# Thirty adaLN blocks go from VectorE to TensorE, and the list that places them is written anew

## The chip, the cores and the metric

The kernel runs on one core of a Trainium2 chip. The metric is the device time of one execution in microseconds (us): the median of the runs. Five engines with instruction streams of their own work side by side: TensorE (PE in the rows; PEld are its weight loads), VectorE (DVE), ScalarE (ACT), GpSimd (POOL) and SyncE (SP), which issues nearly all DMAs of this kernel in order.

## The reference

A two-layer trunk on 256 tokens of 2048 channels, all in float32. Layer 0 is a state-space layer (S5), then keys and values are made once, then layer 1 is attention. Every norm is modulated by the vector `c`: a shift, a scale and, at the end of a layer, a gate, each of 2048 values.

```python
def reference(x, c, ...):
    c_act = silu(c)
    # layer 0
    shift, scale, gate = split(c_act @ mod_w[0] + mod_b[0], 3)
    h = modulate(rmsnorm(x, norm_g[0]), shift, scale)
    x = x + gate * s5_mixer(h, ...)                 # u, z = h @ w_in; scan; GLU; @ w_out
    # shared keys and values
    kv_shift, kv_scale = split(c_act @ kv_mod_w + kv_mod_b, 2)
    h_kv = modulate(rmsnorm(x, kv_norm_g), kv_shift, kv_scale)
    shared = nsa_shared_kv(h_kv, w_kv, ...)         # compressed, selected, window
    # layer 1
    shift, scale, gate = split(c_act @ mod_w[1] + mod_b[1], 3)
    h = modulate(rmsnorm(x, norm_g[1]), shift, scale)
    x = x + gate * nsa_mixer(h, w_qg, w_o, *shared) # queries, gates, attention, @ w_o
    return rmsnorm(x, final_norm_g)
```

The products `c_act @ mod_w` are the adaLN products: 16 blocks of 128 columns for each shift, scale or gate, 128 blocks in all (48 of layer 0, 32 of keys and values, 48 of layer 1). A block is 1 MB of weights that meets one vector.

## The kernel before

**Projections.** A projection (`project`, L231) makes 128 output columns by 256 tokens: 16 weight blocks of 128x128, each split by ScalarE into a high part (`hi`, L202) and by VectorE into the rest (`lo`, L203), and 48 matmuls into one PSUM tile `acc` (L227 to L229). Weights come by SP into `raw` tiles of 512 KB, from a ring of 8 that all weight loads and adaLN loads share.

**adaLN blocks.** Shift and scale of layer 0 are summed by TensorE at the start. The other 96 blocks can go two ways. `pe_mod` takes two blocks (a pair) to TensorE: four DMAs of 512 KB, 32 matmuls of 32 columns into `macc` (L157; the profile has two records for each), a copy by ScalarE (`msum`, L160), two matmuls with ones (L162, four records), two short ScalarE results in `modv`. `dve_mod` takes one block to VectorE: two DMAs of 512 KB (L142) and two halves, each one multiply with a running sum against the broadcast `cact` (L144); the second halves' sums lie in `modw`. `mod_finish` adds the two parts and the bias. `NA, NB = 0, 2` give TensorE 18 blocks (the gate of layer 0 and two of layer 1: 9 pairs) and VectorE 78 (156 halves).

**Stages.** In program order: modulation of layer 0 and half of u; then S5 (the rest of u, the halves of z, `scan_in`, `scan_run`, which is a serial recurrence on VectorE at L608 to L611, `scan_local`, `scan_out`, `y_turn`, for two halves of the channels); GLU (16 projections of `yhl`); output (16 projections of `ghl`; VectorE adds to x at L722 and sums the squares into `tot`, L244); the norm of `x` (`rms_scale`, L247 to L253: a matmul with ones, square root on ScalarE, reciprocal on VectorE, L252) and `norm_mod` to `hkv`; kv (24 projections of `hkv`, the compressions, and the first queries row by row); q (16 projections of queries, the first 4 already made); attention (16 heads, with the z projections between) and the output projection.

**What sets the order.** The Python program is written out by hand, and each engine keeps the order that results. After most steps `fill()` (L555) takes the next string of `PLAN` and does what its letters say: u or z halves, `m` for a pair on TensorE, `d` for a block on VectorE, `c` and `q` for compressions and query rows. What `PLAN` hasn't done in time, loops at the end of a stage do.

Of the kernel before, what the change touches and what calls it, by code (L numbers as in the profile page):

```python
# [8 lines left out]
F32 = mybir.dt.float32  # L9
# [9 lines left out]
KT = 16  # L19
# [18 lines left out]
# columns of the adaLN products, by blocks of 128: 0..47 layer 0, 48..95 layer 1, 96..127 keys and values.  # L38
# Blocks 0..31 come first; of the rest TensorE takes some (weights as they lie) and VectorE the others (turned round).
NA, NB = 0, 2  # L40
# [3 lines left out]
QN = 4    # blocks of the queries that are computed row by row  # L44


def spread(n, slots, a=0):
    """n things over slots a .. slots"""
    r = [0] * slots
    for i in range(n):  # L50
        r[a + i * (slots - a) // n] += 1
    return r


NR = 8    # blocks of u that are computed row by row
SK = 2
# what fills each slot of the program: u, z halves of blocks, m, d modulation (TensorE, VectorE),
# c pieces of the compression, q rows of the queries
PLAN = [
# [4 lines left out]
    "cmd", "mdqq", "dq", "mddq", "dqq", "mdq", "dq", "mddqq", "dq", "mdq", "mqq", "mq", "mq", "d", "d", "",  # L64
    "d", "d", "", "d", "", "", "d", "d", "dd", "d", "", "", "", "d", "d", "d", "", "d", "d", "dd", "", "d",
    "d", "d", "", "d", "dd", "", "",
# [4 lines left out]
def trunk_kernel(ctx, tc, xT, crow, ccol, vec, m0n, mn, mt, w_ur, w_in, w_glu, w_out, w_kv, w_qr, w_q, w_g,  # L71
# [24 lines left out]
    # ---------------------------------------------------------------- constants  # L96
# [34 lines left out]
    # ---------------------------------------------------------------- adaLN products  # L131
    modv = pool.tile([128, 128], F32, name="modv")
    modw = pool.tile([128, 80], F32, name="modw")                     # columns 48 ..
# [41 lines left out]
    # columns of modv: 0..47 layer 0, 48..95 layer 1, 96..127 kv  # L175
    def mod_finish(col, n):
        """Those of the columns col .. col + n that VectorE has summed, in two parts."""
        t = [x for x in range(col, col + n) if x in DVE_MODS]
        if t:
            c = slice(t[0], t[-1] + 1)  # L180
            assert len(t) == t[-1] + 1 - t[0]
            nc.vector.tensor_add(modv[:, c], modv[:, c], modw[:, c.start - 48:c.stop - 48])
            nc.vector.tensor_add(modv[:, c], modv[:, c], vv_("mb", c.start, c.stop))

    # ---------------------------------------------------------------- projections
# [8 lines left out]
    def split_w(r, n):  # L194
        """The first n of the eight blocks in r, four by four."""
# [11 lines left out]
    class Act:  # L207
        """A matrix [2048 channels, 256 tokens] as a high and a low part."""
# [22 lines left out]
    def project(src, act):  # L231
        """The sums [128 columns, 256 tokens]."""
# [13 lines left out]
    def rms_scale(tot):  # L246
        """1 / sqrt(mean square over channels), for every token, on all partitions."""  # L247
# [7 lines left out]
    def norm_mod(xt, rstd, scol, bcol, act, ks=range(KT)):  # L255
        """act = split of (x * rstd) * S + B."""
# [7 lines left out]
    # ---------------------------------------------------------------- layer 0: modulation and u  # L264
    # (the first NR blocks of u, row by row of w_in as the modulation of the rows comes in)
# [38 lines left out]
    # ---------------------------------------------------------------- S5 tables  # L304
# [10 lines left out]
    def exact_exp(dst, src):  # L315
        """e^src to float32's accuracy: 2^k times a polynomial of what is left."""
# [40 lines left out]
    # powers a^1..a^4: [128, 64, 4] real, imaginary  # L357
# [20 lines left out]
    # coef  # L378
# [6 lines left out]
    # coef * a^(3-j): [128, 64, 4]  # L385
# [13 lines left out]
    # a^4 for the chunk recurrence  # L399
# [25 lines left out]
    def outer(dst0, dst1, mr, mi, wr, wi, sub):  # L425
        """dst0 = mr*wr - mi*wi; dst1 = mi*wr + mr*wi, or with sub, mi standing for -mi:
        dst0 = mr*wr + mi*wi; dst1 = mi*wr - mr*wi.  [128, 16 gp, 4, 16]"""
# [13 lines left out]
    for s in (2, 3, 0, 1):  # L441
# [11 lines left out]
        # C a^0 .. C a^3 side by side  # L453
# [5 lines left out]
        # K_d[c_in, c_out] = Re(C a^d Bbar) of the pairs (h = (l, q), b) at partitions (q, b, c_in)  # L459
# [16 lines left out]
        # the input tables turned round, in place: (b, j, c) on partitions, [h, r, g2, n]  # L476
# [12 lines left out]
    # ---------------------------------------------------------------- the rest of u, z, and the scan, in two halves  # L489
    # (halves of the channels; tokens t = 4 k + j are held in the order (j, k) until the end of the layer)  # L490
    ucm = pool.tile([128, KT, 4, 64], F32, tag="zz", name="ucm")
    U = pool.tile([128, KT, 4, 64], F32, tag="uu", name="U")          # (e, j, c), [b, (g2, hl), k]
# [14 lines left out]
    def u_turn(f):  # L507
        """Half of u, (g, e, c) on partitions, to (e, j, c) on partitions."""
# [53 lines left out]
    def scan_in(f):  # L562
        """Inputs of the recurrence over chunks."""
# [38 lines left out]
    def scan_run(f):  # L602
        """The recurrence over chunks."""
# [9 lines left out]
    def scan_local(f, tz):  # L613
        """What comes out of a chunk from its own inputs, in place of U."""
# [14 lines left out]
    def scan_out(f, cts):  # L629
        """The part of y that the states carry, on to U."""  # L630
        VH = VV[f]
        ys = VH[:, 0:8].rearrange("p h r b k -> p (h r b k)").rearrange("p (b g k) -> p b g k", g=4, k=64)
        for q in range(2):
# [10 lines left out]
            for g2 in range(2):  # L644
# [3 lines left out]
                else:  # L648
                    # VectorE is at the recurrence of the other half
# [5 lines left out]
    ycm = U                                                            # (g, e, c), [b, j, k]  # L655

    def y_turn(f):
        """Back to channels (g, e, c) on partitions, through the GELU."""
# [44 lines left out]
    # ---------------------------------------------------------------- GLU  # L703
# [26 lines left out]
    while ndve[0] < 32 - NA:  # L730
        dve_mod()
    mod_finish(96, 32)

    # ---------------------------------------------------------------- shared keys and values
# [46 lines left out]
    def cmp_piece(e, i):  # L781
        """A quarter of the first product of a compression, then the rest of it."""
# [56 lines left out]
    # (queries of the first heads, row by row of their weights as the modulation of the rows comes in)  # L839
# [49 lines left out]
    # masks  # L889
    masks = []  # L890
    for qh in range(2):
# [3 lines left out]
        # cmp: 16 n + 31 <= pos  # L895
# [12 lines left out]
    # gates, token-major [128 tokens, half, (branch, head)]  # L908
# [21 lines left out]
    # half of the gate: the SiLU of z is taken as (1 + tanh(z / 2)) * z, twice its value  # L930
# [10 lines left out]
    # ---------------------------------------------------------------- attention, head by head  # L941
    att = pool.tile([128, 4096], F32, tag="zz", name="att")
    for h in range(16):
        kv = h // 4
        pn = []
        for qh in range(2):
# [12 lines left out]
            # sections: cmp 16 | sel n | win n  # L959
# [22 lines left out]
        # transposed probabilities  # L982
# [36 lines left out]
    # ---------------------------------------------------------------- output projection, final norm  # L1019
# [26 lines left out]
def _lay_out(i):  # L1046
# [10 lines left out]
    def pairs(a):  # L1057
        # groups (b, g2, gpl) -> [g2, (b, gpl), ...]
        return a.reshape((16, 2, 4) + a.shape[1:]).swapaxes(0, 1).reshape((2, 64) + a.shape[1:])
# [30 lines left out]
    lam = np.stack([pairs(i["ssm_lam_re"][0]), pairs(i["ssm_lam_im"][0])])          # [2, g2, gp, n]  # L1090
# [32 lines left out]
```

## Time and profile before

| | |
|---|---|
| device time, median of 3 runs | 1364.43 us (1359.98 to 1368.99) |
| profiled execution: span | 1368.1 us; no time apart from its span is given |
| PE busy | 1267.0 us, 93% |
| VectorE busy | 1068.3 us, 78% |
| ScalarE busy | 681.7 us, 50% |
| DMA | 332.88 MB, mean 243 GB/s |

The profiled span lies 3.7 us above the median and inside the runs. Busy time of PE includes stretches at the lower of its two clock levels; in the rows by window, PEclk is the granted clock as a part of full speed.

### The profile page before, as it was taken

The page shows a single profiled execution, that of the slowest core. Times are in us where ns is not written, and L with a number is a line of the kernel's source. Part 1 is how long each engine was busy: PE and PEld are TensorE (multiplying, and loading weights), DVE is VectorE, ACT ScalarE, POOL GpSimd, SP SyncE. Part 2 cuts the span into 40 slices and gives each one's busy share as a digit, 9 for nine tenths or more (in the row PEclk, how much of TensorE's full clock was granted, in tenths as well). Part 3 has the DMA queues.
Part 4 walks back from the last instruction along what each step waited for, and adds up shares of the span by engine and source line. Part 5 has one row for each costly group of instructions (what it writes and reads, how often), then busy time and mean ns, then how long its engine had stood idle before and what let it go on. Part 6 is the DMA issues. An engine that isn't in the chain of part 4 may idle for free.

```text
span 1368.1 us, 31424 instructions
## 1 busy us (share of the span) xinstructions
PE 1267.0 (93%) x12270; PEld 1200.6 (88%) x12270; DVE 1068.3 (78%) x2612; ACT 681.7 (50%) x1439; POOL 42.5 (3%) x71
## 2 busy tenths in 40 slices
PE   2799979989999999997998999999999999999995
PEld 2678779878888999986997999999999999999995
DVE  5998318999997898889877878776878777777665
ACT  3345544423356555544453545555555555555653
POOL 1000500001001000000000000000000000000001
PEclk9999989999999999997899999999999999999998
DMA  9799966649788999985887888876555444444541
GB/s 359 275 347 336 316 200 200 205 172 336 242 300 299 321 357 318 327 305 187 293 303 248 277 295 289 274 253 227 170 193 194 165 144 141 159 142 161 186 155 62
DMA packets 94055, 332.88 MB, mean 243 GB/s; under 512 B 12785, under 2 KB 13025, under 8 KB 92881
## 3 DMA queue, kind: packets, MB, share of 16 engines
q1 hardware_dynamic: 91792, 321.45, 68.3%
q0 software_dynamic: 2112, 9.42, 2.1%
q8 instruction: 96, 1.57, 0.5%
q14 instruction: 55, 0.44, 0.1%
HBM read 326.10 MB, written 4.72 MB: 242 GB/s over the span
## 4 chain that ended last, share of the span: by engine, by line
PE 68%; DVE 15%; DMA 12%; issue 3%; ACT 2%; SPq 0%; DVEq 0%; ACTq 0%
PE acc L229 18%; PE acc L227 18%; PE acc L228 18%; DMA raw<-in_mt_dram 6%; DVE lo L203 3%; DMA raw<-in_w_in_dram 3%; DVE raw L144 2%; PE macc L157 2%; PE s L957 1%; DVE stab L608 1%; DMA mraw<-in_m0n_dram 1%; PE op L1008 1%; DVE stab L610 1%; PE kp L467 1%; DVE stab L609 1%
## 5 line engine op out<-in xcount | busy, mean ns | idle before, releaser
L202 ACT ACTIVATE hi<-raw 128x512 fp32r<-128x512 f32 x640 | 400.9, 631 | 466.1 <-PE acc L228 395.9
L203 DVE TENSOR_TENSOR lo<-raw,hi 128x512 fp32r<-128x512 f32 x640 | 435.0, 690 | 146.8 <-ACT hi L202 143.6
L228 PE MATMUL acc<-hq,hi 128*128 128x256 f32 x960 | 274.9, 286 | 0.0
L229 PE MATMUL acc<-hq,lo 128*128 128x256 f32 x960 | 271.5, 284 | 2.5 <-DVE lo L203 2.3
L227 PE MATMUL acc<-hq,hi 128*128 128x256 f32 x960 | 273.2, 285 | 0.4 <-ACT hi L202 0.4
L144 DVE SCALAR_TENSOR_TENSOR raw<-raw,cact 128x1024 f32<-128x1024 f32 x156 | 190.1, 1220 | 57.0 <-DMA raw<-in_mt_dram 56.6
L229 PEld LDWEIGHTS acc<-hq,lo 128*128 128x128 f32 x960 | 180.5, 189 | 5.4 <-DVE lo L203 3.9
L228 PEld LDWEIGHTS acc<-hq,hi 128*128 128x128 f32 x960 | 180.9, 188 | 3.7 <-issue 3.3
L227 PEld LDWEIGHTS acc<-hq,hi 128*128 128x128 f32 x960 | 180.9, 188 | 1.3 <-issue 0.7
L229 PE MATMUL acc<-h,lo 128*128 128x256 f32 x384 | 114.0, 297 | 12.7 <-DVE lo L203 12.3
L229 PE MATMUL acc<-hkv,lo 128*128 128x256 f32 x384 | 114.2, 299 | 5.1 <-DVE lo L203 4.6
L227 PE MATMUL acc<-hkv,hi 128*128 128x256 f32 x384 | 112.5, 295 | 4.9 <-ACT hkv L260 4.9
L227 PE MATMUL acc<-h,hi 128*128 128x256 f32 x384 | 113.5, 296 | 1.0 <-ACT hi L202 1.0
L228 PE MATMUL acc<-hkv,hi 128*128 128x256 f32 x384 | 111.9, 294 | 0.8 <-DVE hkv L261 0.8
L228 PE MATMUL acc<-h,hi 128*128 128x256 f32 x384 | 111.6, 291 | 0.0
L229 PEld LDWEIGHTS acc<-h,lo 128*128 128x128 f32 x384 | 76.1, 198 | 17.4 <-DVE lo L203 14.0
L229 PEld LDWEIGHTS acc<-hkv,lo 128*128 128x128 f32 x384 | 77.3, 202 | 7.6 <-DVE lo L203 7.2
L227 PEld LDWEIGHTS acc<-hkv,hi 128*128 128x128 f32 x384 | 77.3, 202 | 5.8 <-ACT hkv L260 5.8
L227 PEld LDWEIGHTS acc<-h,hi 128*128 128x128 f32 x384 | 76.1, 198 | 5.3 <-issue 2.5
L228 PEld LDWEIGHTS acc<-hkv,hi 128*128 128x128 f32 x384 | 77.4, 202 | 1.4 <-DVE hkv L261 1.4
L157 PE MATMUL macc<-mraw,cz 128*32 128x128 f32 x1600 | 59.0, 300 | 18.9 <-DMA mraw<-in_m0n_dram 17.9
L228 PEld LDWEIGHTS acc<-h,hi 128*128 128x128 f32 x384 | 76.1, 198 | 0.1
(312 smaller groups left out, 2829.6 us busy)
## 6 DMA issues: line engine op xcount, KB each, us to landing
raw<-in_mt_dram SPq DMA_DIRECT2D x156, 512.0 KB, 5.6
raw<-in_w_z_dram SPq DMA_DIRECT2D x96, 512.0 KB, 3.7
mraw<-in_m0n_dram SPq DMA_DIRECT2D x64, 512.0 KB, 7.8
raw<-in_w_in_dram SPq DMA_DIRECT2D x48, 512.0 KB, 6.1
raw<-in_w_kv_dram SPq DMA_DIRECT2D x48, 512.0 KB, 5.2
mraw<-in_mn_dram SPq DMA_DIRECT2D x36, 512.0 KB, 6.6
raw<-in_w_glu_dram SPq DMA_DIRECT2D x32, 512.0 KB, 6.3
raw<-in_w_out_dram SPq DMA_DIRECT2D x32, 512.0 KB, 6.1
```

The costliest lines, as they stand in the source:

```text
L144: nc.vector.scalar_tensor_tensor(out=rf, in0=rf, scalar=1.0, in1=cact[:, 1024 * e:1024 * e + 1024], op0=OP.mult, op1=OP.mult, accum_out=mo ...
L157: nc.tensor.matmul(acc[32 * j:32 * j + 32, 128 * e:128 * e + 128], cz[:, q, :], r[:, q % 8, :], start=(e == 0 and q < 4), stop=(q >= 12), ...
L202: nc.scalar.activation(hi[:, 0:c, :], rr, AF.Copy)
L203: nc.vector.tensor_sub(lo[:, 0:c, :], rr, hi[:, 0:c, :].bitcast(F32))
L227: nc.tensor.matmul(acc, hi[:, kk, :], act(0, k), start=(k == 0), stop=False)
L228: nc.tensor.matmul(acc, hi[:, kk, :], act(1, k), start=False, stop=False)
L229: nc.tensor.matmul(acc, lo[:, kk, :], act(0, k), start=False, stop=(k == KT - 1))
L467: nc.tensor.matmul(kp[32 * q:32 * q + 32, l, :], bb[r][pr, 32 * h:32 * h + 32], kc_[pr, 2 * h:2 * h + 2, r, :], start=(l == 0 and r == 0), ...
L608: V.tensor_mul(ra, VH[:, :, :, :, k], ar)
L609: V.tensor_mul(rb, VH[:, :, ::-1, :, k], ai)
L610: V.tensor_add(ra, ra, VH[:, :, :, :, k + 1])
L957: nc.tensor.matmul(sp, qo(a, h)[:, qs], kk[:, kv, b, o:o + w], start=(i == 0), stop=(i == 2))
```

## The change

It moves the 32 blocks of the keys and values to TensorE, and the two of layer 1 that TensorE had back to VectorE: 48 blocks (24 pairs) on TensorE, 48 (96 halves) on VectorE. `PLAN` is new throughout. Two statements ahead of the norm of keys and values, which the kernel before needed for blocks on VectorE, are gone. All else in the diff are comments that are removed; line numbers rise by one.

```diff
-NA, NB = 0, 2
+NA, NB = 32, 0
 L1 = [t for k in range(16) for t in (48 + k, 64 + k)]
 PE_MODS = list(range(32, 48)) + list(range(96, 96 + NA)) + L1[:NB]
 DVE_MODS = list(range(96 + NA, 128)) + L1[NB:] + list(range(80, 96))
...
 PLAN = [
-    "zzm", "", "um", "u", "d", "z", "z", "d", "m", "z", "zu", "zz", "dm", "m", "zm", "zmz", "z", "mz", "zzzz",
-    "", "dzzmz", "dzz", "zz", "zd", "zz", "", "dd", "dzmd", "d", "zd", "", "mmm", "m", "", "dd", "d", "d",
...
+    "zzm", "m", "um", "mu", "m", "z", "zm", "m", "m", "z", "zum", "zz", "m", "m", "zm", "zmz", "z", "mz", "zzzz",
+    "", "zz", "zzm", "zz", "z", "zz", "", "m", "zmz", "", "zm", "", "", "m", "", "m", "", "", "m", "", "", "m",
+    "", "", "", "", "", "", "",
+    "m", "d", "m", "d", "m", "d", "m", "d", "", "d", "", "d", "", "d", "", "d", "",
...
 ]
...
     while npe[0] < 16 + NA:
         pe_mod()
-    while ndve[0] < 32 - NA:
-        dve_mod()
-    mod_finish(96, 32)
```

What the letters come to, by stage:

| stage | pairs on TensorE before, after | blocks on VectorE before, after |
|---|---|---|
| S5 | 9, 18 | 12, 0 |
| GLU | 0, 4 | 14, 0 |
| output | 0, 2 | 10, 8 |
| kv | 0, 0 | 26, 25 |
| q | 0, 0 | 10, 0 |
| attention | 0, 0 | 6, 15 |

SP at the start of S5: the loads of w_in (projections) and of the adaLN products. `in_mn` holds blocks for TensorE, four loads to a pair, `in_mt` those for VectorE, two to a block. Before:

```order
L190 DMA raw<-in_w_in_dram 128x1024 x2
L155 DMA mraw<-in_mn_dram 128x1024 x4
L190 DMA raw<-in_w_in_dram 128x1024
L155 DMA mraw<-in_mn_dram 128x1024 x4
L190 DMA raw<-in_w_in_dram 128x1024 x15
L142 DMA raw<-in_mt_dram 128x1024 x2
L190 DMA raw<-in_w_in_dram 128x1024 x2
L142 DMA raw<-in_mt_dram 128x1024 x2
L155 DMA mraw<-in_mn_dram 128x1024 x4
L190 DMA raw<-in_w_in_dram 128x1024 x4
L142 DMA raw<-in_mt_dram 128x1024 x2
L155 DMA mraw<-in_mn_dram 128x1024 x8
```

The same place in the changed kernel:

```order
L191 DMA raw<-in_w_in_dram 128x1024 x2
L156 DMA mraw<-in_mn_dram 128x1024 x8
L191 DMA raw<-in_w_in_dram 128x1024
L156 DMA mraw<-in_mn_dram 128x1024 x8
L191 DMA raw<-in_w_in_dram 128x1024 x15
L156 DMA mraw<-in_mn_dram 128x1024 x4
L191 DMA raw<-in_w_in_dram 128x1024 x2
L156 DMA mraw<-in_mn_dram 128x1024 x12
L191 DMA raw<-in_w_in_dram 128x1024 x2
L156 DMA mraw<-in_mn_dram 128x1024 x4
L191 DMA raw<-in_w_in_dram 128x1024 x2
L156 DMA mraw<-in_mn_dram 128x1024 x8
```

The pairs ahead of the rest of u are four in place of two, and pairs stand where VectorE's blocks were.

TensorE at `scan_in` of the second half, before: `vp` are the inputs of the recurrence, the 32 `macc` rows are a pair's matmuls (three of them stand apart, above).

```order
L229 MATMUL acc<-h_160,lo 128x256
L623 MATMUL tp<-U,cbS 64x64 x16
L573 MATMUL vp_3398<-U,Vvb 64x64 x16
L573 MATMUL vp_3399<-U,Vvb 64x64 x16
L157 MATMUL macc<-mraw,cz 32x128 x29
L573 MATMUL vp_3482<-U,Vvb 64x64 x15
L162 MATMUL macc<-ones,msum 128x1 x2
L573 MATMUL vp_3482<-U,Vvb 64x64
L573 MATMUL vp_3483<-U,Vvb 64x64 x16
```

The same place after:

```order
L230 MATMUL acc<-h_160,lo 128x256
L158 MATMUL macc<-mraw,cz 32x128 x32
L624 MATMUL tp<-U,cbS 64x64 x16
L574 MATMUL vp_3621<-U,Vvb 64x64 x3
L163 MATMUL macc<-ones,msum 128x1 x2
L574 MATMUL vp_3621<-U,Vvb 64x64 x13
L574 MATMUL vp_3622<-U,Vvb 64x64 x7
L158 MATMUL macc<-mraw,cz 32x128 x32
L574 MATMUL vp_3622<-U,Vvb 64x64 x9
L574 MATMUL vp_3705<-U,Vvb 64x64 x7
L163 MATMUL macc<-ones,msum 128x1 x2
```

Where the matmuls and the sum of one pair stood among the `vp` matmuls, those of two stand. In the GLU stage, which held projections alone, pairs now stand between the projections' matmuls; one of them, after:

```order
L228 MATMUL acc<-yhl_5295,hi 128x256
L229 MATMUL acc<-yhl_5295,hi 128x256
L230 MATMUL acc<-yhl_5295,lo 128x256
L158 MATMUL macc<-mraw,cz 32x128 x32
L228 MATMUL acc<-yhl_5294,hi 128x256
L229 MATMUL acc<-yhl_5294,hi 128x256
L230 MATMUL acc<-yhl_5294,lo 128x256
```

VectorE from the end of the output stage to the reciprocal of the norm, before (`x` is the last sum of the stage, `tot` the last sum of squares; the L144 rows are halves of layer 1's blocks):

```order
L144 SCALAR_TENSOR_TENSOR raw,modw<-raw,cact 128x1024
L722 SCALAR_TENSOR_TENSOR x<-acc,modv,x 128x256
L203 TENSOR_TENSOR lo<-raw,hi 128x512
L859 SCALAR_TENSOR_TENSOR scol_8201<-modv,vecs 128x1
L244 TENSOR_TENSOR tot<-tot,sq 128x256
L144 SCALAR_TENSOR_TENSOR raw,modv<-raw,cact 128x1024
L144 SCALAR_TENSOR_TENSOR raw,modw<-raw,cact 128x1024
L252 RECIPROCAL rstd<-rstd 128x256
L857 TENSOR_TENSOR modv<-modv,modw 128x2
```

The same place after:

```order
L723 SCALAR_TENSOR_TENSOR x<-acc,modv,x 128x256
L204 TENSOR_TENSOR lo<-raw,hi 128x512
L145 SCALAR_TENSOR_TENSOR raw,modv<-raw,cact 128x1024
L245 TENSOR_TENSOR tot<-tot,sq 128x256
L145 SCALAR_TENSOR_TENSOR raw,modw<-raw,cact 128x1024
L855 TENSOR_TENSOR modv<-modv,modw 128x2
L856 TENSOR_TENSOR modv<-modv,vecs 128x2
L857 SCALAR_TENSOR_TENSOR scol_8736<-modv,vecs 128x1
L253 RECIPROCAL rstd<-rstd 128x256
L260 SCALAR_TENSOR_TENSOR xn<-x,scol,rstd 128x256 x4
L145 SCALAR_TENSOR_TENSOR raw,modv<-raw,cact 128x1024
```

Before, a half stands ahead of the last `x` and two behind the last `tot`; after, one stands between `x` and `tot` and one behind `tot`, with the three short sums of a finished block.

## Rows read from the trace of the kernel before

**Rows 1.** The page, part 1: busy us, share, instructions of each engine.
```profile
PE 1267.0 (93%) x12270; PEld 1200.6 (88%) x12270; DVE 1068.3 (78%) x2612; ACT 681.7 (50%) x1439; POOL 42.5 (3%) x71
```

**Rows 2.** By window: length, busy us of each engine, PEclk, DMA share, GB/s; S5 to attention.
```profile
184.00:424.00 240.00, 223.32 (x2941) 200.67 (x2942) 206.09 (x684) 109.20 (x204) 11.49 (x19) 0.93 0.70 241
424.00:521.00 97.00, 95.55 (x787) 94.44 (x786) 86.09 (x158) 53.28 (x97) 0.00 (x0) 1.00 0.93 329
521.00:612.50 91.50, 91.43 (x770) 91.19 (x768) 78.12 (x150) 47.74 (x84) 0.00 (x0) 1.00 0.90 312
612.50:625.00 12.50, 1.28 (x3) 0.56 (x3) 10.67 (x21) 1.98 (x5) 0.00 (x0) 0.59 0.90 312
625.00:848.00 223.00, 210.59 (x1620) 203.75 (x1620) 181.47 (x366) 109.96 (x215) 0.00 (x0) 0.94 0.78 266
848.00:925.00 77.00, 74.30 (x602) 72.18 (x602) 60.38 (x134) 42.13 (x90) 0.00 (x0) 1.00 0.80 274
925.00:1261.00 336.00, 336.00 (x2710) 326.71 (x2710) 254.94 (x718) 185.78 (x474) 0.00 (x0) 1.00 0.51 169
```

**Rows 3.** By window, line 144 alone (x counts halves twice): S5, GLU, output, q.
```profile
184.00:424.00 240.00, 29.30 (x48) 0.93 0.70 241
424.00:521.00 97.00, 36.45 (x59) 1.00 0.93 329
521.00:612.50 91.50, 27.41 (x46) 1.00 0.90 312
848.00:925.00 77.00, 17.31 (x30) 1.00 0.80 274
```

**Rows 4.** By window, line 157 alone: S5, 64 records to a pair.
```profile
184.00:424.00 240.00, 17.33 (x512) 14.73 (x512) 0.93 0.70 241
```

**Rows 5.** Timeline of PE around one pair: start, us, line, names, count.
```profile
365.21 0.28 PE L229 MATMUL acc<-h,lo 128*128 128x256 f32 x1
365.42 1.96 PE L157 MATMUL macc<-mraw,cz 128*32 128x128 f32 x64
367.31 0.39 PE L227 MATMUL acc<-h,hi 128*128 128x256 f32 x1
...
370.02 0.28 PE L228 MATMUL acc<-h,hi 128*128 128x256 f32 x1
370.13 0.50 PE L162 MATMUL macc<-ones,msum 128*128 128x1 f32 x4
370.50 0.36 PE L229 MATMUL acc<-h,lo 128*128 128x256 f32 x1
```

**Rows 6.** Timeline of PE in S5: its longest idle times, in brackets with releaser.
```profile
186.02 1.02 PE L162 MATMUL macc<-ones,msum 128*128 128x1 f32 x4 [7.05 <-ACT msum L160]
...
236.12 0.58 PE L229 MATMUL acc<-h,lo 128*128 128x256 f32 x1 [2.44 <-DVE lo L203]
...
285.68 0.58 PE L229 MATMUL acc<-h,lo 128*128 128x256 f32 x1 [4.25 <-DVE lo L203]
...
349.44 0.58 PE L229 MATMUL acc<-h,lo 128*128 128x256 f32 x1 [3.26 <-DVE lo L203]
```

**Rows 7.** Timeline of VectorE just before the second of these.
```profile
234.22 1.23 DVE L144 SCALAR_TENSOR_TENSOR raw<-raw,cact 128x1024 f32<-128x1024 f32 x1 [3.22 <-DMA raw<-in_mt_dram]
```

**Rows 8.** Timeline of VectorE at the norm behind output.
```profile
617.31 0.48 DVE L722 SCALAR_TENSOR_TENSOR x<-acc,modv,x 128x256 f32<-128x256 f32 x1
...
619.66 1.23 DVE L144 SCALAR_TENSOR_TENSOR raw<-raw,cact 128x1024 f32<-128x1024 f32 x1 [0.86 <-DMA raw<-in_mt_dram]
...
620.93 1.23 DVE L144 SCALAR_TENSOR_TENSOR raw<-raw,cact 128x1024 f32<-128x1024 f32 x1
...
622.08 1.75 DVE L252 RECIPROCAL rstd<-rstd 128x256 f32<-128x256 f32 x1
```

**Rows 9.** Timeline of PE at the same place.
```profile
612.15 0.28 PE L229 MATMUL acc<-ghl,lo 128*128 128x256 f32 x1
618.85 1.22 PE L249 MATMUL rsum<-tot,ones 128*128 128x256 f32 x2 [6.42 <-DVE tot L244]
```

More of the change, by code (lines that the diff above doesn't have):

```diff
@@ L59 @@
 PLAN = [
[4 rows of a table removed]
-    "cmd", "mdqq", "dq", "mddq", "dqq", "mdq", "dq", "mddqq", "dq", "mdq", "mqq", "mq", "mq", "d", "d", "",
-    "d", "d", "", "d", "", "", "d", "d", "dd", "d", "", "", "", "d", "d", "d", "", "d", "d", "dd", "", "d",
-    "d", "d", "", "d", "dd", "", "",
[8 rows of a table added]
 ]
```

6 rows, old and new, of the table PLAN are left out of this document.

## The prediction

> **What bounds the kernel now.** I read the busy shares first: PE works 93% of the span, VectorE 78% [rows 1]. Then the same by stage [rows 2], because the change touches some stages only. Three kinds are to be seen there. In output and attention PE has no idle time at all (91.43 of 91.50 us, 336.00 of 336). In GLU and q it has a little (1.5 and 2.7 us). In S5 and at the norm behind output it has most of what this change could reach: 16.7 us of 240, and 11.2 of 12.5. VectorE is at 80 to 90% in S5, GLU and output, so it looks nearly full, but only where PE waits for it does that cost time.
>
> S5's loss is larger than its idle time. The granted clock is 0.93 on the mean [rows 2]. With two levels, full and half, that is 14% of 240 us, about 34 us, at the lower one. At most 17 of these are the idle time; the other 17 are work at half rate, which would have taken 8.5. So S5 loses about 25 us against a PE that never waits (estimate). Four of its idle times are 17.0 us in sum [rows 6]: one is ScalarE's copy `msum`, three are `lo` of VectorE. Of these three, one stands behind an adaLN half that waited 3.22 us for its data [rows 7]; the other two, 4.25 and 3.26 us, fall while VectorE is in the serial recurrence.
>
> GLU: its window has 787 matmul records; output does 770 in 91.5 us, 0.119 us each [rows 2]. At that pace GLU needs 93.7 of its 97.0 us and loses 3.3.
>
> **Part 1: what a pair costs on PE.** The last projection matmul before a pair starts at 365.21, so the next was due 0.119 later, at 365.33; it starts at 367.31: 1.98 us. The sum displaces, from 370.14 to 370.50, 0.36 more [rows 5]. That is 2.34 us a pair with a clock at full rate. Over S5 the 64 records take 17.33 / 8 = 2.17 us [rows 4], which includes some at the lower clock, and would make 2.5. I take 2.4. Fifteen more pairs are +36 us of PE: nine in S5 +21.6, four in GLU +9.6, two in output +4.8. ScalarE's three short copies for each lie beside other work (it is at 50%), with one reservation that is rival B.
>
> A pair also changes the shape that TensorE multiplies in, 32 columns in place of 128. The row shows the price: where one projection matmul follows another it starts 0.16 us before the other's end, and here the projection starts 0.07 before the end of the pair [rows 5], so 0.09 us a change. The Trainium skill speaks against this change at that point ("TensorEngine Tiling (Array Packing)", Tiling Modes, Key Properties): changing the tiling mode drains TensorE. The trace agrees, and the drain lies inside the 2.34 us; by the rule alone, 2 to 4 changes for each of 15 pairs at 0.09 us would be 3 to 5 of the 36 us, not something on top.
>
> **Part 2: what VectorE is given back.** Thirty blocks are 60 halves. In S5 29.30 us of them go, in GLU 36.45, in output about a fifth of 27.41, in q 17.31 [rows 3]; attention takes over about ten blocks, 20 halves of 1.23 us [rows 8], +24.6 us. What this is worth is bounded by the PE losses above, stage by stage:
> - S5: bounds 0 and 25. All 24 halves leave, 15 us of them inside the recurrences by the letters, so `lo` comes up earlier and the wait of rows 7 can't happen. On the other side the recurrence itself stays, and PE has 21.6 us more to do while it runs, which fills idle time that was VectorE's. The order shows pairs put among the `vp` matmuls, where PE waited. But the first idle time (7.05) has nothing to do with VectorE. I take 14: a little over half. S5 +7.6.
> - GLU: bounds 0 and 3.3. All its halves leave, with VectorE at 89% before; I take 3. GLU +6.6.
> - Output: it loses nothing, so nothing can be recovered. +4.8.
> - q: bounds 0 and 2.7; I take 2.5, since VectorE goes from 78% to 56% there.
> - kv: 26 blocks become 25, its idle 12.4 us stay. 0.
>
> **Part 3: the norm behind output.** PE ends its last projection at about 612.4 [rows 9]. VectorE reaches the last x only at 617.31, because halves of layer 1, one of them waiting for data, stand ahead; `rsum` starts at 618.85; two more halves hold the reciprocal until 622.08 [rows 8, 9]. In the new order x comes directly, then one `lo` and one half before `tot`, one half and three short sums before the reciprocal. At row prices: x from 612.5, `tot` about 614.8, `rsum` 615.2 and 1.2 long, reciprocal about 617. That is 5 us; the half's data can be late (0.86 us was waited for one here, rows 8). Bounds 0 and 6 (no half at all); I take 4.
>
> **Part 4: attention.** VectorE goes from 255 to 280 of 336 us, 83%, at a PE that never waits. No row shows that stage at that load. The nearest: output at 85% loses 0.1 us, GLU at 89% loses 3.3 of 97, which would be 11 of 336 [rows 2]. Output is nearer; since a head's softmax is a serial chain on VectorE and a half in it delays it, I take +2.
>
> **Sum.** S5 +7.6, GLU +6.6, output +4.8, norm -4, q -2.5, kv 0, attention +2: +14.5 us. Against the profiled execution that is 1368.1 + 14.5 = 1382.6; this execution lies 3.7 above the median, so the forecast is 1364.4 + 14.5 = **1379 us**.
>
> **Rivals.**
>
> A: VectorE is the true bound from S5 on, and PE's losses all go. For it: VectorE at 86% in S5, three of four long idle times end with `lo`. Against: two of them fall in the recurrence, which stays. It would give S5 21.6 - 25 = -3.4, GLU +6.3, output +4.8, norm -6, q -2.7, attention 0: -1.0, **1363 us**, not slower. It decides from S5: if more than 22 of the 25 us go there, the stage is no longer longer than before.
>
> B: weights late at the start of S5. Four pairs, not two, are loaded ahead of the rest of u: 8 more loads of 512 KB, 4.2 MB, through the one queue and the 8 buffers; at 329 GB/s, the best of a stage [rows 2], 12.7 us. ScalarE waits for a weight tile, its copy `msum` queues behind that, PE stands at the sum, and all projections queue behind that, as at 186.02 for 7.05 us [rows 6]. For it: this happened at just this place. Against: S5 as a whole moves 241 GB/s, and would go to about 276 with the pairs' 8.4 MB more, so there is room. All of the 12.7 us on the path: **1392 us**.
>
> C: nothing is recovered in S5, because its idle times belong to the recurrence and the data, and PE's longer work merely comes on top: +14 on the forecast, **1393 us**. For it: the first, third and fourth of rows 6. Against: PE work that needs no VectorE now lies beside the recurrence.
>
> That the change does something else than it says is excluded by the order of the instructions, which shows the pairs and halves where the letters put them.
>
> **How the numbers follow.** Forecast 0.58, with a range of its own of 1370 to 1388 from the bounds of S5 (give or take 7), attention and norm; A 0.17; B 0.13; C 0.12. The range of 8 in 10 reaches to A's time and to B's, with half of A's spread below it and half of C's above: 1363 to 1392. A measurement of this kernel can tell about 1% from no change, so the bounds are 1350.8 and 1378.1. The forecast lies on the upper one: half of it, 0.30, with B and C gives slower 0.55; the other half and nearly all of A same 0.43; faster 0.02, since even with every loss recovered the 36 us are only just paid.
>
> **What would show it.** Right: the records of the pairs' matmuls rise by 960, PE's busy time by 25 to 30 us (36 less what a higher clock gives back); output grows by 4 to 5 us; in GLU PE's waits for `lo` vanish and the stage still grows; `rsum` starts 2 to 3 us behind the last projection in place of 6.4; VectorE's busy time falls by 60 halves of 1.22 us, 73 us, all stages to output and q losing it and attention gaining it. Wrong in S5: waits of PE for `msum` (B), or the same waits for `lo` at the recurrences at the same length (C), or a stage shorter than 240 us (A). The prediction is wrong as a whole if a pair on PE costs far less than 2.34 us, because its matmuls fill time in which PE would have waited anyway, in GLU and output too.

## The result, and the profile after

The changed kernel takes 1411.13 us, the median of four runs (1410.32 to 1413.92), against 1364.88 (1359.98 to 1368.99): a ratio of 1.034, 95% interval 1.032 to 1.036. Its profiled execution spans 1409.8 us, 41.7 more than that of before. The direction was forecast, 1379 was not: the time lies 19 us above the range.

The page of the changed kernel, part 1, and from part 5 the groups of the halves and of the pairs' matmuls (line, names, count, busy us, mean ns, idle before):

```profile
PE 1291.6 (92%) x13290; PEld 1224.7 (87%) x13290; DVE 1004.4 (71%) x2492; ACT 689.7 (49%) x1484; POOL 41.3 (3%) x71
...
L145 DVE SCALAR_TENSOR_TENSOR raw<-raw,cact 128x1024 f32<-128x1024 f32 x96 | 117.3, 1221 | 51.9 <-DMA raw<-in_mt_dram 51.7
...
L158 PE MATMUL macc<-mraw,cz 128*32 128x128 f32 x2560 | 91.0, 294 | 29.1 <-DMA mraw<-in_m0n_dram 19.1
```

These numbers are close to those foreseen: 960 more records of pairs, PE busy for 24.6 us more than in [rows 1], VectorE for 64 us less (73 were foreseen). So of the 41.7 us by which the span grew, 24.6 are busy time of PE, which the forecast had. The other 17.1 are time in which PE has no work; the forecast had that time fall by 10 to 16 us, and what it missed lies there.

By stage (first group of columns as in [rows 2]: S5, GLU, output, norm, kv, and q with attention):

```profile
184.00:458.60 274.60, 248.83 (x3699) 224.52 (x3700) 183.87 (x642) 115.89 (x234) 10.26 (x19) 0.92 0.70 239
458.60:560.80 102.20, 102.20 (x1042) 100.88 (x1041) 55.02 (x96) 55.04 (x108) 0.00 (x0) 1.00 0.74 253
560.80:666.20 105.40, 99.22 (x907) 96.36 (x905) 75.08 (x147) 48.76 (x89) 0.00 (x0) 1.00 0.84 288
666.20:679.50 13.30, 1.39 (x4) 0.50 (x2) 11.08 (x23) 2.07 (x5) 0.00 (x0) 0.69 0.88 326
679.50:889.00 209.50, 199.06 (x1567) 193.67 (x1568) 170.77 (x345) 108.32 (x212) 0.00 (x0) 0.95 0.75 259
889.00:1302.00 413.00, 413.00 (x3363) 403.20 (x3362) 319.31 (x860) 228.93 (x564) 0.00 (x0) 1.00 0.58 195
```

I cut both traces at the same events, the first or last matmul on each activation (on `hq` the first of the gates and projections; the row-by-row queries stand in kv). Worked out from these times, rounded to 0.1 us:

| stage, from event to event | before | after | measured | forecast |
|---|---|---|---|---|
| start and S5, to the first GLU matmul | 423.2 | 458.7 | +35.5 | +7.6 |
| GLU, to the first output matmul | 97.8 | 102.2 | +4.4 | +6.6 |
| output, to its last matmul | 91.2 | 105.2 | +14.0 | +4.8 |
| norm, to the first kv matmul | 12.7 | 13.4 | +0.7 | -4 |
| kv, to the first matmul on `hq` | 212.6 | 209.7 | -2.9 | 0 |
| q and attention, to the last matmul on `hq` | 422.8 | 412.9 | -9.9 | -0.5 |
| rest | 107.8 | 107.8 | 0 | 0 |

One cut isn't clean. In the kernel before, 32 matmuls of keys, values and row-by-row queries stand behind the first one on `hq`, after none. At 0.119 us each they are 3.8 us; counted with kv, they make kv +0.9 and q and attention -6.1.

S5 is where most of it lies. That stage varies between executions: four kernels with the same program up to the end of S5 as the kernel before (itself and three below) reached the first GLU matmul at 423.2, 431.9, 420.8 and 425.5 us. Against their mean of 425.4 the changed kernel is 33 us late, and a second kernel with its S5 (output's blocks moved, below) came at 458.0. Between single profiles, a difference of less than some 11 us in S5 says little by itself.

The timeline of PE in S5 after: the rows that begin behind its three longest idle times (in brackets), to be held against [rows 6]:

```profile
184.34 0.91 PE L574 MATMUL vp<-U,Vva 64*64 64x64 f32 x12 [12.22 <-ACT U L519]
...
288.65 1.72 PE L158 MATMUL macc<-mraw,cz 128*32 128x128 f32 x28 [8.10 <-ACT modv L166]
...
373.84 0.58 PE L230 MATMUL acc<-h,lo 128*128 128x256 f32 x1 [9.21 <-DVE lo L204]
```

29.5 us in three waits, where [rows 6] had 17.0 in four. The second can be followed through three engines. SP's issues (start, us from the first to the last of the row, and the count):

```profile
228.45 8.49 SPq L156 DMA_DIRECT2D mraw<-in_mn_dram  x4
239.52 3.24 SPq L191 DMA_DIRECT2D raw<-in_w_in_dram  x2
245.15 28.15 SPq L156 DMA_DIRECT2D mraw<-in_mn_dram  x12
276.51 0.92 SPq L191 DMA_DIRECT2D raw<-in_w_in_dram  x2
277.52 11.94 SPq L156 DMA_DIRECT2D mraw<-in_mn_dram  x4
```

SP issues 12 loads for pairs in a row, which takes it from 245.15 to 273.30, and only then the next weights of `w_in`, at 276.51. The ring has 8 tiles; a tile of a pair is free only when PE has reached its matmuls, and PE is busy with other work ahead of them. The largest of SP's own waits from 240 to 277 us (us in total, times, longest) is for that:

```profile
SPq L156 <- PE macc L158: 18.7, 4, 8.8
```

What the DMA engines do meanwhile (by window; the last two columns are the DMA share and GB/s):

```profile
266.00:273.00 7.00, 7.00 (x135) 6.46 (x135) 6.52 (x30) 1.32 (x3) 0.00 (x0) 1.00 0.06 19
273.00:278.00 5.00, 5.00 (x154) 4.65 (x152) 4.66 (x22) 1.43 (x5) 0.57 (x1) 1.00 0.91 306
278.00:289.00 11.00, 2.90 (x82) 2.66 (x80) 8.96 (x35) 3.72 (x9) 0.00 (x0) 0.68 0.89 352
```

Between 266 and 273 us the DMA engines all but stand still (0.06 busy, 19 GB/s), not because there is nothing to load but because no tile is free for it. When the weights are issued at last, ScalarE's timeline shows who waits for them:

```profile
277.88 0.39 ACT L161 ACTIVATE msum<-macc 128x256 f32<-128x256 f32 x1 [2.80 <-PE macc L158]
285.15 1.15 ACT L203 ACTIVATE hi<-raw 128x512 fp32r<-128x512 f32 x2 [6.88 <-DMA raw<-in_w_in_dram]
286.21 1.05 ACT L579 ACTIVATE Vvb<-vp 128x504 f32<-128x504 f32 x2
287.15 1.15 ACT L203 ACTIVATE hi<-raw 128x512 fp32r<-128x512 f32 x2
288.19 0.41 ACT L166 ACTIVATE modv<-macc,vecs 128x1 f32<-128x1 f32 x2
```

ScalarE waits 6.88 us for `w_in`; the pair's `modv` copies, which could have been made from 279.3 on, when PE had ended the pair's sum, stand behind in its order and come at 288.19. The next pair can't start before (there is one `macc` tile), and everything on PE stands behind that pair: 8.10 us, and then some at the lower clock (0.68 in the window from 278 to 289). The first wait, 12.22 us, at the place of rival B, is the same chain on ScalarE, with a copy to `U` behind late weights. But what makes them late is another thing. SP's issue, ScalarE's rows, and a window:

```profile
160.47 0.33 SPq L191 DMA_DIRECT2D raw<-in_w_in_dram  x1
...
183.17 0.63 ACT L203 ACTIVATE hi<-raw 128x512 fp32r<-128x512 f32 x1 [15.40 <-DMA raw<-in_w_in_dram]
183.71 0.58 ACT L519 ACTIVATE U<-ut 128x512 f32<-128x512 f32 x1
...
172.00:176.00 4.00, 0.12 (x2) 0.00 (x0) 0.00 (x0) 0.00 (x0) 0.63 (x1) 1.00 1.00 183
```

These weights were issued at 160.47 and used 23 us later. Until 176 the DMA engines were busy all the time, at only 183 GB/s in the last 4 us, with the pairs' loads that stand ahead and with GpSimd's own (`cact`, `cbS`). So here the transfers themselves were late, not the free tile.

The third wait begins when `lo` stands among the steps of a recurrence that has started 24.6 us later than before (last `vp` matmul at 305.4 against 280.8).

Output has another cause. Waits in the output stage after (us in total, times, longest):

```profile
DVE raw L145 <- DMA raw<-in_mt_dram: 18.7, 10, 4.8
...
PE acc L230 <- DVE lo L204: 6.1, 8, 1.8
```

Before, VectorE waited 1.8 us for such data in that stage. And at the norm, the timelines of VectorE and of PE, to be held against [rows 8, 9]:

```profile
668.41 1.22 DVE L145 SCALAR_TENSOR_TENSOR raw<-raw,cact 128x1024 f32<-128x1024 f32 x1
...
670.23 0.48 DVE L723 SCALAR_TENSOR_TENSOR x<-acc,modv,x 128x256 f32<-128x256 f32 x1
...
673.25 1.23 DVE L145 SCALAR_TENSOR_TENSOR raw<-raw,cact 128x1024 f32<-128x1024 f32 x1 [1.95 <-DMA raw<-in_mt_dram]
...
674.40 0.42 DVE L245 TENSOR_TENSOR tot<-tot,sq 128x256 f32<-128x256 f32 x1
674.74 1.22 DVE L145 SCALAR_TENSOR_TENSOR raw<-raw,cact 128x1024 f32<-128x1024 f32 x1
...
676.64 1.75 DVE L253 RECIPROCAL rstd<-rstd 128x256 f32<-128x256 f32 x1
```

```profile
674.88 1.22 PE L250 MATMUL rsum<-tot,ones 128*128 128x256 f32 x2 [8.51 <-DVE tot L245]
```

The rows of the order that I went by begin at the last x; halves stand ahead of it too, and the next one waits for its data. The last x comes at 670.23, 3.9 us behind the end of PE's last matmul (666.37), the matmul of the sum 8.51 behind, and the reciprocal 10.3.

### The profile page after: what moved, and what is told of

It is laid out like the page before. It is cut to its first block, busy times and chain, and to the rows that moved or that the text cites. A ratio compares the mean times of both kernels' runs of the same rounds, so it can differ in the third digit from the quotient of the medians.

```text
span 1409.8 us, 33378 instructions
## 1 busy us (share of the span) xinstructions
PE 1291.6 (92%) x13290; PEld 1224.7 (87%) x13290; DVE 1004.4 (71%) x2492; ACT 689.7 (49%) x1484; POOL 41.3 (3%) x71
## 4 chain that ended last, share of the span: by engine, by line
PE 72%; DMA 11%; DVE 11%; ACT 3%; issue 2%; SPq 0%; DVEq 0%; ACTq 0%
PE acc L230 18%; PE acc L228 18%; PE acc L229 18%; DMA raw<-in_mt_dram 5%; DMA raw<-in_w_in_dram 4%; PE macc L158 4%; DVE lo L204 2%; DVE raw L145 2%; DMA mraw<-in_m0n_dram 2%; PE s L955 1%; PE op L1006 1%; PE vp L574 1%; PE kp L468 1%; ACT hi L203 1%; DVE Vvb L612 1%
## 5 line engine op out<-in xcount | busy, mean ns | idle before, releaser
L145 DVE SCALAR_TENSOR_TENSOR raw<-raw,cact 128x1024 f32<-128x1024 f32 x96 | 117.3, 1221 | 51.9 <-DMA raw<-in_mt_dram 51.7
L158 PE MATMUL macc<-mraw,cz 128*32 128x128 f32 x2560 | 91.0, 294 | 29.1 <-DMA mraw<-in_m0n_dram 19.1
L158 PEld LDWEIGHTS macc<-mraw,cz 128*32 128x32 f32 x2560 | 74.3, 118 | 38.7 <-issue 20.6
L228 PEld LDWEIGHTS acc<-h,hi 128*128 128x128 f32 x384 | 74.7, 195 | 9.3 <-ACT hi L203 4.7
```

Source lines behind the costliest of these rows:

```text
L145: nc.vector.scalar_tensor_tensor(out=rf, in0=rf, scalar=1.0, in1=cact[:, 1024 * e:1024 * e + 1024], op0=OP.mult, op1=OP.mult, accum_out=mo ...
L158: nc.tensor.matmul(acc[32 * j:32 * j + 32, 128 * e:128 * e + 128], cz[:, q, :], r[:, q % 8, :], start=(e == 0 and q < 4), stop=(q >= 12), ...
L228: nc.tensor.matmul(acc, hi[:, kk, :], act(0, k), start=(k == 0), stop=False)
```

## The experiments

Ten kernels ran, beside runs of the kernel before on the same chip. The stage times below are cut as in the table above. Theory 1 says that the added loss comes from data: pairs' loads that hold the ring in S5, halves of VectorE that wait for theirs in output and at the norm. Theory 2 says that it is TensorE's own time for the pairs.

**The added pairs without loads.** In `pe_mod_pair`:

```diff
-                if q % 8 == 0:
+                if q % 8 == 0 and not added:
                     r = raw_tile("mraw")
...
-                nc.tensor.matmul(acc[...], cz[:, q, :], r[:, q % 8, :],
+                nc.tensor.matmul(acc[...], cz[:, q, :], ident if added else r[:, q % 8, :],
```

> The changed kernel, but the 15 added pairs (every second one of the 18 in S5, all four in GLU, both in output) multiply a constant tile that lies in SBUF: their 60 loads are left out, all matmuls, copies and sums stay. Theory 1 (in S5 the pairs' loads hold the ring of 8 tiles and SP's queue, so the projections' weights come late): S5 loses its long idle times, 15 to 25 us shorter; output 3 to 6 us shorter; about 1385 us. Theory 2 (the time is TensorE's own for the pairs): S5 as long as before, about 1408 us.

1396.2 us (1393.3 to 1397.6). The first GLU matmul comes at 433.5 in place of 458.7: S5 is 25 us shorter, at the upper end of theory 1. The waits of PE in S5 that are left (releaser, us in total, times, longest):

```profile
PE acc L231 <- DVE lo L205: 7.9, 3, 5.4
...
PE macc L158 <- issue: 4.2, 2, 2.9
...
PE macc L163 <- ACT msum L161: 3.2, 1, 3.2
```

None is above 5.4 us, and none is for `modv`; the wait for U, just ahead of this window, was 2.7 us in place of 12.2. Output stayed at 104.5, so its loss is not that of the pairs' loads; that part of the expectation missed. kv was 11 us longer than in the changed kernel, with the same letters, which is why the time fell by 15 and not by 25, to half way between what the two theories expected.

**The added pairs with fewer matmuls.**

```diff
                 j = q % 4
+                if added and q not in (0, 1, 2, 3, 8):
+                    continue
```

> The changed kernel, but the 15 added pairs do 10 of their 32 matmuls (the product is incomplete); all loads stay. That takes 22/32 of 1.96 us, 1.35 us a pair, 20 us in all from TensorE. Theory 1 (data): S5 hardly shorter, 0 to 6 us, since the loads hold the ring as before; GLU 5.4 and output 2.7 us shorter; about 1400 us. Theory 2 (TensorE's own time): the whole 20 us go, about 1391 us or less.

1388.0 us (1386.0 to 1396.4; the profiled execution was the slowest of them, 1396.4). The time is the one that theory 2 expected. In that profile S5 is 7.3 us shorter, just beyond theory 1's limit and within the stage's spread, GLU 3.6. What tells the theories apart is PE's idle time from 160 us to the first GLU matmul: 35.6 us here, 37.7 in the changed kernel, 18.0 without the loads. Fewer matmuls leave the waits as they were. Output fell by 8.0, more than its pairs' matmuls (2.7): VectorE's waits for data there were 6.3 us in place of 18.7. I can't say why the data were in time here. The median went down by 23 us, more than the matmuls' 20. The three faster executions have no profile, so where they gained isn't known, and by its time this run speaks for theory 2.

**Pairs spread among the weights.** The letters of S5:

```diff
-    "zzm", "m", "um", "mu", "m", "z", "zm", "m", "m", "z", "zum", "zz", "m", "m", "zm", "zmz", "z", "mz", "zzzz",
-    "", "zz", "zzm", "zz", "z", "zz", "", "m", "zmz", "", "zm", "", "",
+    "zzm", "", "um", "u", "zm", "z", "zm", "z", "zm", "z", "zum", "z", "zm", "z", "zm", "zzm", "z", "zm", "zzm",
+    "z", "zzm", "zm", "zm", "zm", "zm", "z", "", "zm", "", "", "", "zm",
```

> The changed kernel with the same 18 pairs and 29 halves of z in S5, but the letters of S5 alternate, so that no two pairs follow each other in SP's queue without one or two weight loads between (before, up to three pairs, 12 loads, stood together); GLU and all behind as they were. Theory 1 (trains of pairs fill the ring of 8): the waits for w_in at 172 and 280 us get shorter, S5 10 to 20 us shorter, about 1396 us. Theory 2 (TensorE's own time): no change, 1411 give or take 4.

1405.4 us (1393.5 to 1408.7). The last `vp` matmul comes at 293.1 in place of 305.4 and the first `yt` at 350.8 in place of 381.2, and PE's wait for U fell from 12.2 to 1.7 us. But pairs now stand late in S5, and 22 of those 30 us were lost again behind (from the first to the last `yt` 84.0 us, in the changed kernel 62.0). Eight us were left at the end of S5: half of what was expected, and within the stage's spread. The waits for the pairs' copies did not shrink: `msum` and `modv` cost PE 14.4 us, in the changed kernel 12.4. So trains of pairs in SP's queue are not the whole of it.

**Nine pairs in S5, the rest in GLU and output.** Letters alone: S5 has the pairs of the kernel before and none of its VectorE blocks, GLU nine pairs, output six and no VectorE blocks, kv eight blocks more.

> The changed kernel with S5's pairs back at nine, in the slots of the kernel before and with none of VectorE's blocks; nine pairs in GLU, six in output, no VectorE blocks in output, eight more in kv. Theory 1 (the added pairs cost S5 their 21.6 us and some 25 more through their loads): S5 ends at 408 to 423 us of the profile, GLU 116, output 105, in all 1370 to 1382 us. Theory 2 (a pair costs 2.4 us of TensorE wherever it stands, and no more): S5, GLU and output together as long as in the changed kernel, 1400 to 1411 us.

1411.3 us (1409.3 to 1418.5). S5 ends at 407.0, as theory 1 wants: the stage (by window) is 223 us long with PE busy for 214.70 and a granted clock of 0.97.

```profile
184.00:407.00 223.00, 214.70 (x2989) 193.72 (x2989) 177.63 (x633) 107.30 (x200) 10.20 (x19) 0.97 0.59 203
```

Up to the last output matmul 26 us are saved (640.0 against 666.1), which speaks against theory 2. But 24 of them were lost again: kv took 231.1 us in place of 209.7, and the norm 15.9 in place of 13.4, so the time is 29 us above theory 1's range. I put that down to the eight blocks moved into kv. No run shows them apart, and kv took 225.3 us in a kernel without them (below). GLU with nine pairs took 122.7 and output with six 110.3 us: 24.9 and 19.1 above the kernel before, 2.8 and 3.2 us a pair.

**VectorE's relief alone.** The kernel before, where `dve_mod` passes over the first twelve blocks.

> The kernel before with the twelve blocks that VectorE sums in S5 left out, loads and halves (their columns are set to zero). It measures what S5 gets back from VectorE's relief alone, without pairs. The forecast's step: 14 us. If S5's idle time belongs to the recurrence and to the weights' arrival: 0 to 4 us. The time: 1350 against 1361 to 1365.

1354.2 us (1351.8 to 1358.5), a ratio of 0.992 (0.988 to 0.995). S5 ends at 406.1, 17 us earlier than in the profile before and 19 earlier than the mean of the four. So the relief was worth what the forecast gave it, 14, and a little more; that S5 gets nothing back (rival C) falls, for a kernel without the added pairs. The run takes away 24 loads along with the halves, and doesn't say which of the two gave the time back.

**The blocks of output moved to GLU.** The letters of the output stage; eight of GLU's empty slots get a `d`:

```diff
-    "m", "d", "m", "d", "m", "d", "m", "d", "", "d", "", "d", "", "d", "", "d",
+    "m", "", "m", "", "m", "", "m", "", "", "", "", "", "", "", "", "",
```

> The changed kernel with the eight blocks that VectorE sums in the output stage moved to GLU, where it has none. Theory 1 (in output and at the norm VectorE stands in halves whose data come late, and lo and x queue behind): output falls from 105 to 96 or 97 us (91.3 and two pairs), the norm from 13.4 to 7 to 10, GLU stays at 102 to 104; 1411 falls to 1396 to 1400 us. Theory 2 (output's length is the two pairs' own, whatever VectorE does): output stays at 103 to 105, 1408 to 1411 us.

1405.9 us (1403.9 to 1409.4). Output took 97.7 us in place of 105.2, and VectorE's waits for data in it fell from 18.7 us to

```profile
DVE raw L145 <- DMA raw<-in_mt_dram: 3.5, 5, 1.4
```

as theory 1 says; GLU 104.4. The norm stayed at 13.1, a miss, and the time fell by 5 us, not by 11 to 15. The halves that stand in the norm here are not those of output. They come from the first letters of kv, and VectorE's order holds them ahead of the sum.

**The pairs' copies on VectorE.**

```diff
-        nc.scalar.activation(sm, acc[:, 0:256], AF.Copy)
+        nc.vector.tensor_copy(sm, acc[:, 0:256])
...
-            nc.scalar.activation(modv[:, cols[e]:cols[e] + 1], acc[:, 256 + e:257 + e], AF.Identity,
-                                 bias=vv_("mb", cols[e], cols[e] + 1))
+            nc.vector.tensor_add(modv[:, cols[e]:cols[e] + 1], acc[:, 256 + e:257 + e],
+                                 vv_("mb", cols[e], cols[e] + 1))
```

> The changed kernel with the pairs' short copies (msum and the two columns of modv) on VectorE in place of ScalarE; loads and matmuls stay. Theory 1a (PE waits because these copies stand behind a hi that waits for weights in ScalarE's order): the waits of PE for msum and modv in S5, 12 us, go, and S5 is 10 to 15 us shorter, about 1398 us. Theory 1b (the weights are late in any case, and PE would wait for lo or hi next): 0 to 4 us, 1407 to 1411.

1401.7 us (1398.7 to 1403.6), S5 11 us shorter: nearer to 1a. The waits of PE in S5 for the copies became

```profile
PE macc L166 <- DVE msum L162: 7.1, 5, 3.8
...
PE acc L234 <- ACT hi L209: 5.1, 4, 2.4
```

7.1 us where `msum` and `modv` had cost 12.4, and 5.1 for `hi`. The wait for U at 12 us stayed (11.4). The largest fall is in a wait that theory 1a doesn't name: `lo`, from 9.9 to 2.4 us. So part of the cost of late weights lies in who stands behind them on ScalarE, and part stays whatever the order there.

**Two kernels with the head of the kernel before.** Their letters behind the norm came from the changed kernel; first all of them, then only those of q and attention.

> The kernel before up to the norm behind output (its NA, NB and its letters), with the changed kernel's letters from there on: 25 blocks in kv, none in q, one for each head of attention. In the changed kernel kv to the last query or z projection was 13 us shorter. If that comes from the letters behind the norm: 1352 us. If it comes from VectorE's being ahead there, or from work that the earlier stages took over: 1362 to 1368 us.

1370.8 us (ten runs, 1366.2 to 1379.0; the profiled execution was the slowest), ratio 1.004 (1.002 to 1.007). From the first matmul on `hq` it gained what was looked for (412.7 against 422.8), and kv lost it again (225.3 against 212.6). The second has, of the letters of q (first row) and attention, only these changed:

```diff
-    "d", "d", "", "d", "d", "", "d", "", "", "d", "d", "dd", "d", "", "", "",
-    "d", "d", "d", "", "d", "d", "dd", "", "d", "d", "d", "", "d", "dd", "", "",
+    "", "", "", "", "", "", "", "", "", "", "", "", "", "", "", "",
+    "d", "d", "d", "d", "d", "d", "d", "d", "d", "d", "d", "d", "d", "d", "d", "d",
```

> The kernel before with only the letters of q and attention changed: its ten blocks in q and six in attention become one for each of the 16 heads. In five kernels with these letters the stretch from the last kv matmul to the last query or z matmul took 413 us, against 421.5. If the letters of q and attention do it: 1356 us. If something is taken from kv for it, as in the run with kv's letters changed as well: 1364 to 1371.

1361.3 us (ten runs, 1356.0 to 1368.0), ratio 0.996 (0.993 to 0.998): q and attention 414.3, kv 214.2. The median fell by 5.6 us against the runs beside it, two thirds of the 8.5.

**The norm cleared.** On top of that, letters of output (first row) and of kv's first twelve slots:

```diff
-    "d", "m", "m", "d", "dmd", "", "d", "", "dm", "d", "", "d", "dm", "", "d", "",
-    "mdd", "dm", "d", "m", "mdcd", "dcm", "cdd", "dcd", "cd", "cmd", "cd", "cmd",
+    "d", "md", "m", "d", "dmd", "", "d", "", "dm", "d", "", "d", "dm", "", "", "",
+    "m", "m", "", "m", "mddcd", "ddcm", "cdd", "dcd", "cd", "cdd", "cd", "cdd",
```

> The kernel r8_tail2 (the kernel before with the sixteen last blocks one to a head) with the blocks around the norm moved: the last block of output goes to its second slot, those of kv's first four slots to its fifth to twelfth. No half of an adaLN block stands any more among VectorE's last x and tot and the reciprocal. If the halves are what holds the norm: from the last output matmul to the first of hkv 12 us become 6 to 8, and the time 1361 becomes 1356. If the norm's own chain (sum, square root, reciprocal, scaling) sets it: 11 to 13 us as before, 1361.

1353.9 us (six runs, 1351.1 to 1354.9), ratio 0.990 (0.988 to 0.993): faster than both kernels, by 1% than the one before. Its norm took 6.1 us in place of 12.7. VectorE's timeline there, to be held against [rows 8]:

```profile
613.82 0.48 DVE L723 SCALAR_TENSOR_TENSOR x<-acc,modv,x 128x256 f32<-128x256 f32 x1
614.36 0.69 DVE L204 TENSOR_TENSOR lo<-raw,hi 128x512 fp32r<-128x512 f32 x1
614.97 0.42 DVE L245 TENSOR_TENSOR tot<-tot,sq 128x256 f32<-128x256 f32 x1
616.68 1.75 DVE L253 RECIPROCAL rstd<-rstd 128x256 f32<-128x256 f32 x1 [1.30 <-ACT rstd L252]
618.47 1.67 DVE L260 SCALAR_TENSOR_TENSOR xn<-x,scol,rstd 128x256 f32<-128x256 f32 x4
```

## Why the prediction was wrong

Right were the direction and the bound of it: PE's added work is not paid for by VectorE's relief.

**The step that failed is the price of a pair in S5** (part 1: "I take 2.4 ... nine in S5 +21.6"). It holds PE's own time for a pair and puts the pair's loads at nothing. The term beside it held: with nine pairs and no VectorE blocks S5 ended at 407.0 or 406.1, 16 to 19 us earlier, where I had taken 14. From there, nine more pairs led to 458.7: 51.7 us, 5.7 a pair. Without their loads it is 433.5: 26.5 us, 2.9 a pair, near the 2.34 that I had read. From 160 us to the first GLU matmul (columns as in [rows 2]), the changed kernel, the one without the loads, and the one with nine pairs:

```profile
160.00:458.70 298.70, 261.05 (x3819) 231.32 (x3818) 184.57 (x643) 119.23 (x240) 15.41 (x28) 0.91 0.71 235
160.00:433.50 273.50, 255.47 (x3795) 228.72 (x3788) 184.10 (x642) 121.05 (x238) 13.78 (x25) 0.95 0.57 188
160.00:407.00 247.00, 229.11 (x3222) 202.43 (x3214) 179.65 (x637) 112.18 (x209) 14.71 (x27) 0.96 0.62 206
```

The nine pairs' matmuls add 26.4 us of busy time and no idle time (18.0 against 17.9). The loads add the other 25 us: 19.6 of idle time, and 5.6 of busy time at a granted clock of 0.91 in place of 0.95. Where the traces let it be followed, the weights behind the pairs' loads in SP's order come late, for want of a free tile or of DMA time; ScalarE waits for them, and PE waits for ScalarE's copies. Matmuls and loads don't add up exactly: with loads and 10 of 32 matmuls S5 was still 44 us longer than with nine pairs.

Rival B named this chain and put it at one place, the start, at 12.7 us. The 12.22 us wait at that place is in the profile; but the kernel before had 2.1 and 7.05 us there, so the start alone costs little more. What B missed is that the chain comes back later in S5, as at 288.65, and there by the full ring. The argument against it, that the stage as a whole has room for 276 GB/s, was an average: the stage moved 239 GB/s in the end, with 7 us at 19 in it. Its sum was off as well: by the table, 36 loads more and 24 fewer are 6.3 MB, not 8.4.

The idle time of S5 was read from rows that don't match. The four times of [rows 6] are 17.0 us in sum, but 5.0 of the first lie ahead of 184, where the window with its 16.7 us of idle time begins; 4.7 of that window are shorter waits.

**Output and norm** (+14.0 and +0.7 against +4.8 and -4). In part 2 "it loses nothing, so nothing can be recovered" was right, and I did not ask what it could newly lose. With the blocks gone from output the stage was 97.7 us, so 7.5 of the 9 us too much are halves whose data come late, each holding `lo` and `x` behind it; the rest is pairs at 3.2 us rather than 2.4. For the norm I counted the halves from the last x on, priced them at 1.23 us each, and allowed 1 us for late data. The halves ahead of the last x, which my rows left out, held it to 670.23, and a later one waited 1.95 us. That halves set the norm's length is shown by the run that cleared it: 6.1 us.

**GLU** was right in kind, +4.4 for +6.6. **Attention and q** were a term of the wrong size, -9.9 (or -6.1, with the cut put right) for -0.5; attention's +2 is not borne out. From the first to the last matmul on `hq`, ten kernels with one block to each head and none in q took 412.7 to 414.3 us, the two with blocks in q 422.8 and 420.9. VectorE's additional 22 us of halves in attention (nine blocks by the table, where I wrote about ten) cost nothing that can be seen. That q's own blocks had cost more than the 2.7 us of idle time in its window is likely but not shown apart, since the letters of q and attention changed together.

**Open.** kv took from 207.8 to 225.3 us in kernels with nearly the same letters there. Its longer cases have more waits of VectorE for adaLN data (35.6 us at 225.3, 14.1 at 207.8), but what sets whether these are in time I haven't settled. How much of the loads' 25 us in S5 belongs to the full ring, and how much to busy DMA engines as at the start, is open too: no kernel with a larger ring ran.

## What to carry to other kernels

Price work that is moved to another engine with the buffers that it holds and the queue in which its loads stand, not with the engine's time alone: here a pair's loads cost S5 about as much again as its matmuls. A stage's mean DMA rate can hide that there is no room when loads are issued in order into a shared ring (7 us at 19 GB/s in a stage of 239); look for stretches in which the DMA engines stand still while the issuing queue waits. And an instruction that waits for data in an in-order engine ahead of a serial step (here a half ahead of the sum and the reciprocal) can cost that step its whole wait: moving five letters away from it gained 7 us.

## What the runs showed of the hardware

The DMA engines moved next to nothing from 266 to 273 us in the changed kernel (0.06 busy, 19 GB/s), although loads were outstanding in the program, because the queue that issues them stood at a load without a free tile. From 172 to 176 us they were busy all the time and moved 183 GB/s, so a full busy share was not a full rate. ScalarE's order passes a single late tile on: 6.88 us of wait for one weight tile became 8.10 us on PE through a copy of 0.41 us.
